# A hybrid decoder block on one core: adaLN's first part as TensorE products in column groups, and S5 without GpSimd

## The chip, the core and the metric

The kernel runs on one core of a Trainium2 chip. TensorE multiplies matrices into PSUM, VectorE (DVE) and ScalarE (ACT) do element work on SBUF and PSUM, GpSimd (POOL) does element work on SBUF alone, and SyncE (SP) issues most of the DMAs. Engines run side by side; each takes its own instructions in order. The metric is the device time of one execution in microseconds, as the median of several runs.

## The reference

One layer (sequence 512, model width 1024, batch 1) of a token mixer and a channel mixer. Cut to what the change touches:

```python
c_act = jax.nn.silu(c)
mod = c_act @ ada_w + ada_b                       # (1024) @ (1024 x 6144)
sh1, sc1, gt1, sh2, sc2, gt2 = split(mod, 6)
h = rms_norm(x, pre1_w) * (1.0 + sc1) + sh1       # sh1, sc1: "adaLN's first part"
z = h @ w_in                                      # one input projection for three branches
#  A: chunked gated linear attention   B: mLSTM   C: S5, a complex diagonal state space
y = (g0 * (A @ proj_gla) + g1 * (B @ proj_ml) + g2 * (C @ proj_s5)) @ w_out
x = x + (1.0 + gt1) * rms_norm(y, post1_w)
#  then the channel mixer: SwiGLU with its own shift, scale and gate
```

In S5 each group of 16 channels drives 64 complex states, `x_t = Abar x_{t-1} + Bbar u_t`, `y_t = Re(C x_t) + D u_t`, with `Abar` and `Bbar` computed from `lam`, `log_step` and `b`.

## The kernel before, in words

Large matrix products keep fp32's precision by splitting each operand into a `hi` half (rounded, on ScalarE) and a `lo` half (what is left, on VectorE or GpSimd) and adding three products: hi by hi, hi by lo, lo by hi (`passes`, lines 424 to 426; for products with tokens on the partitions, lines 456 to 458). Weights come through one stream (`Stream`): SP loads an item into a `raw` buffer (line 321), and `S.ahead(i, n)` splits the items up to `i + n`. In the opening the ring has nine raw buffers, later three.

The opening is laid out by hand: inside `head` the order on all engines is the order of the text, though small work of later stages (S5's parameters, named `w`) is put into it by the planner, which places all other instructions by its own costs and by the order in which they were written. The opening does this:

- TensorE runs products of ones by ones (`warm`, line 542, counts in `WARM`) while x comes in. The squares of x are summed, `r` is the reciprocal root, and `rb` its broadcast over partitions in PSUM (line 573).
- adaLN's first part has a matrix of 1024 by 2048, in 16 loads of 512 KB. The columns are cut into five `STRIPS` of 128 or 256. A load holds two or four slices along the contraction. Some loads (`NA` of each strip) are scaled on ScalarE and added on GpSimd (`ada_act`), the others are accumulated on VectorE (`ada_acc`); both end in an `acc` of 128 partitions.
- `prep(j)` sums `acc` over the partitions by products with a column of ones (line 589, and 591 for strip 0), which gives the scale and shift of the strip as columns, and forms `h` and the halves `hT` of its normed input from x, the columns and `rb`.
- `sweep(j)` multiplies the strip's `hT` into six PSUM banks (eight slices of the contraction in all, six groups of three products each). After `SWN[j]` groups it prepares the next strip.

Then follow the linear attention (seven levels of block masks, on VectorE, lines 1073 to 1097), S5 and mLSTM. Their own work is small, and large projections (`job`, run in pieces by `fill(n)`) stand between their steps, so that TensorE has work while the other engines prepare. S5's parameters (`s5_params`) give `bb` (a complex product on GpSimd) and the table of phases `ph` (one half of the columns on VectorE, the other on GpSimd). S5 runs over four blocks of eight groups: `params(b)` forms outer products (`outer`: of four products `o` two are VectorE's, two GpSimd's), sums them to `CA` and `wp`, multiplies small matrices in column groups of 32 (line 1239) and transposes; `states(b)` multiplies the inputs into states (line 1268), rotates them by `ph` (four products on VectorE, two adds on GpSimd), runs two scans on VectorE, rotates back (four products on GpSimd) and sums to `Xs`; `outputs(b)` gives the outputs. `rho` is copied to a tile on GpSimd.

After that come the merge of the branches, the output projection and the channel mixer, which the change doesn't touch.

Of the kernel before, what the change touches and what calls it, by code (L numbers as in the profile page):

```python
# [9 lines left out]
OP = mybir.AluOpType  # L10
# [5 lines left out]
STRIPS = ((0, 128), (1, 256), (3, 256), (5, 256), (7, 128))  # L16
# [150 lines left out]
PP = (1, 3, 5)  # L167
WARM = (17, 1, 2, 0, 7, 0, 7)
LEAD = 5
AB = (0, 0, 0)  # L170
NA = (1, 2, 2, 2, 1)
SWN = (3, 5, 5, 5, 0)
# [14 lines left out]
def _emit(tc, nc, ctx, ExitStack, A, out, act, dve, pool, pe, sp):  # L187
# [286 lines left out]
    def ada_act(dst, k0, n, more):  # L474

        def f(t):
            w = 1024 // n
            for i in range(n):
                sl = slice(i * w, (i + 1) * w)
                af(t[:, sl], t[:, sl], AF.Copy, scale=cact[:, k0 + i:k0 + i + 1])  # L480
            if n == 4:
                tt(pool, t[:, 0:512], t[:, 0:512], t[:, 512:1024], OP.add)
            a = dst()
            if more:
                tt(pool, t[:, 0:w], t[:, 0:w], t[:, w:2 * w], OP.add)
                tt(pool, a, a, t[:, 0:w], OP.add)
            else:
                tt(pool, a, t[:, 0:w], t[:, w:2 * w], OP.add)
        return f

    cact2 = const.tile([128, 8], F32, name="cact2")
    adas = {}
    strip_w, strip_a = [], []
    i = 0
    for j, (c0, w) in enumerate(STRIPS):
        n = 512 // w
        na = NA[j]
        strip_a.append(len(items))
        for z in range(8 // n):
            def dst(j=j, z=int(z >= na), w=w):  # L500
                if (j, z) not in adas:
                    adas[j, z] = slot("acc")
                return adas[j, z][:, 0:2 * w]

            def other(j=j, w=w):
                return adas[j, 0][:, 0:2 * w]

            add_item(A["ada0"][i], kind="ada", start=True,
                     acc=ada_act(dst, n * z, n, z > 0) if z < na else
                     ada_acc(dst, n * z, n, n * na, None, other if j else None))  # L510
            i += 1
        strip_w.append([add_item(A["sweep"][k], w=768, start=True, pool=k in PP) for k in range(c0, c0 + w // 128)])

# [23 lines left out]
    af(st[:, 0:1], epsc, AF.Sqrt)  # L537
# [8 lines left out]
    for i in range(4):  # L546
        warm(WARM[i], ones)
        sq = [slot("sq"), slot("sq")]
        for h in range(2):
            xh = xT[i][:, h * 512:(h + 1) * 512]  # L550
            if h and i == 2:
# [22 lines left out]
    warm(WARM[5], ones)  # L574
    S.ahead(1, 0)
# [3 lines left out]
    S.ahead(2, 0)  # L579
    S.ahead(strip_a[1] + NA[1] - 1, 0)  # L580
    sweep_ps = [mm_bank() for _ in range(4)] + [ax_bank() for _ in range(2)]

    def prep(j):
# [13 lines left out]
        for k in range(c0, c0 + n):  # L597
            hs[k] = slot("h")
            hT[k] = tuple(hTp.tile([128, 512], F32R, tag=f"{z}{k}", name="hT") for z in "hl")
            stt(hs[k], xT[k // 2][:, (k % 2) * 512:(k % 2 + 1) * 512], g1c[:, k:k + 1], rb, OP.mult, OP.mult)  # L600
            af(hT[k][0], hs[k], AF.Identity, bias=s1c[:, k:k + 1])
        for k in range(c0, c0 + n):
            stt(hT[k][1], hs[k], s1c[:, k:k + 1], hT[k][0].bitcast(F32), OP.add, OP.subtract)

    def sweep(j):

        for i, idx in enumerate(strip_w[j]):
            k = STRIPS[j][0] + i
# [245 lines left out]
    with head:  # L854
        prep(0)
        warm(WARM[6], ones)
# [874 lines left out]
```

## Time and profile before

| | us |
|---|---|
| runs | 949.90, 950.78, 953.11 |
| median | 950.78 |
| profiled execution | 952.81 |
| its span, first to last instruction | 950.9 |

The profiled execution is one of its own, and the rows below come from it. Times in it are microseconds from the start of its span. "Busy" is the time in which an engine has at least one instruction; TensorE's products overlap, so a product of 0.39 us can follow the one before it after 0.23. PEclk is the share of 2.4 GHz that was granted to TensorE; 0.50 is 1.2 GHz. DVE is VectorE, ACT ScalarE, POOL GpSimd, PE TensorE, SPq the DMA issues of SyncE.

### The profile page before, as it was taken

The numbers are of one execution on the slowest core, as the hardware profiler recorded it, in microseconds if no ns is written. First come the engines' busy times: TensorE is split into PE (matmuls) and PEld (weight loads), VectorE is DVE, ScalarE is ACT, GpSimd is POOL, SyncE is SP. The second block draws the span as 40 slices with busy tenths as digits, with TensorE's granted clock in tenths as the row PEclk, the third lists the DMA queues.
The fourth block names the chain that finished last, engine by engine and source line by source line (L and its number), as shares of the span: only waits on it lengthen the run. The fifth ranks groups of instructions, "written<-read, shape, count | busy, mean of one in ns | idle before, by whom it ended". The sixth has DMA issues, their size and how long they took to land.

```text
span 950.9 us, 11658 instructions
## 1 busy us (share of the span) xinstructions
PE 908.7 (96%) x4290; PEld 741.8 (78%) x4290; DVE 606.4 (64%) x1100; ACT 337.8 (36%) x519; POOL 168.8 (18%) x208
## 2 busy tenths in 40 slices
PE   9699999999888999999999998999999999999997
PEld 9577787777776787878888786788888888888885
DVE  4998998889798894595667779653343433322215
ACT  5338513432323444362333354522322323212113
POOL 4440005405235230221212223000000000000000
PEclk7799999999999999999999999999999999999999
DMA  9624242133433432243555733444243333333303
GB/s 365 218 81 130 90 144 66 35 113 112 148 112 112 127 110 78 89 137 108 177 175 167 237 131 133 154 156 132 89 141 126 110 108 114 111 97 104 110 1 133
DMA packets 52193, 120.80 MB, mean 127 GB/s; under 512 B 13796, under 2 KB 19428, under 8 KB 52136
## 3 DMA queue, kind: packets, MB, share of 16 engines
q1 hardware_dynamic: 49944, 115.92, 37.1%
q0 software_dynamic: 1040, 2.38, 1.0%
q10 hardware_dynamic: 1152, 1.75, 0.5%
q8 instruction: 34, 0.56, 0.3%
q14 instruction: 23, 0.19, 0.1%
HBM read 113.21 MB, written 6.82 MB: 126 GB/s over the span
## 4 chain that ended last, share of the span: by engine, by line
PE 51%; DVE 7%; DMA 3%; issue 1%; ACT 1%; POOL 0%; SPq 0%; DVEq 0%; ACTq 0%
PE mm L424 11%; PE mm L425 11%; PE mm L426 11%; PE y L1512 4%; PE y L1513 4%; PE y L1511 4%; DVE lo L222 1%; DMA raw<-ada 1%; DVE xn L228 1%; PE mm L456 1%; PE mm L457 1%; PE mm L458 1%; DVE st L228 1%; DVE xn L222 1%; DMA raw<-wout 1%
## 5 line engine op out<-in xcount | busy, mean ns | idle before, releaser
L231 ACT ACTIVATE hi<-raw 128x1024 fp32r<-128x1024 f32 (+2 forms) x157 | 151.7, 971 | 406.1 <-PE mm L425 161.0
L222 DVE TENSOR_TENSOR lo<-raw,hi 128x1024 fp32r<-128x1024 f32 (+2 forms) x151 | 180.9, 1200 | 163.7 <-ACT hi L231 163.1
L424 PE MATMUL mm<-h2hi,hi 128*128 128x512 f32 x320 | 124.7, 390 | 0.0
L426 PE MATMUL mm<-h2hi,lo 128*128 128x512 f32 x320 | 124.6, 389 | 0.0
L425 PE MATMUL mm<-h2lo,hi 128*128 128x512 f32 x320 | 124.5, 389 | 0.0
L426 PE MATMUL mm<-hT,lo 128*128 128x512 f32 x280 | 112.9, 403 | 9.2 <-DVE lo L222 9.2
L424 PE MATMUL mm<-hT,hi 128*128 128x512 f32 x280 | 114.0, 407 | 0.0
L425 PE MATMUL mm<-hT,hi 128*128 128x512 f32 x280 | 112.6, 402 | 0.3 <-DVE hT L228 0.3
L426 PEld LDWEIGHTS mm<-hT,lo 128*128 128x128 f32 x280 | 54.4, 194 | 22.3 <-DVE lo L222 10.5
L426 PEld LDWEIGHTS mm<-h2hi,lo 128*128 128x128 f32 x320 | 60.1, 188 | 12.6
L425 PEld LDWEIGHTS mm<-h2lo,hi 128*128 128x128 f32 x320 | 60.1, 188 | 12.4
L424 PEld LDWEIGHTS mm<-h2hi,hi 128*128 128x128 f32 x320 | 60.1, 188 | 12.3
L1513 PE MATMUL y<-hi,g 128*128 128x512 f32 x176 | 68.5, 389 | 0.0
L1512 PE MATMUL y<-lo,g 128*128 128x512 f32 x176 | 68.5, 389 | 0.0
L1511 PE MATMUL y<-hi,g 128*128 128x512 f32 x176 | 68.3, 389 | 0.0
L222 DVE TENSOR_TENSOR sg<-sg,mm 128x512 f32<-128x512 f32 x36 | 24.7, 685 | 67.7 <-PE mm L426 67.7
L425 PEld LDWEIGHTS mm<-hT,hi 128*128 128x128 f32 x280 | 54.6, 195 | 12.5 <-DVE hT L228 1.1
L424 PEld LDWEIGHTS mm<-hT,hi 128*128 128x128 f32 x280 | 54.7, 195 | 12.0 <-issue 0.5
L228 DVE SCALAR_TENSOR_TENSOR gacc<-raw,cact,gacc 128x512 f32<-128x512 f32 x56 | 45.0, 803 | 21.7 <-DMA raw<-ada 21.0
L456 PE MATMUL mm<-hi,hT 128*128 128x512 f32 x128 | 50.5, 401 | 2.3 <-ACT mo L231 2.3
L457 PE MATMUL mm<-lo,hT 128*128 128x512 f32 x128 | 50.0, 391 | 0.0
L458 PE MATMUL mm<-hi,hT 128*128 128x512 f32 x128 | 49.5, 392 | 0.0
(322 smaller groups left out, 1598.0 us busy)
## 6 DMA issues: line engine op xcount, KB each, us to landing
raw<-ada SPq DMA_DIRECT2D x48, 512.0 KB, 3.4
raw<-ffn SPq DMA_DIRECT2D x44, 512.0 KB, 3.4
raw<-wzg SPq DMA_DIRECT2D x24, 512.0 KB, 3.4
raw<-ffo SPq DMA_DIRECT2D x22, 512.0 KB, 3.2
raw<-wpr SPq DMA_DIRECT2D x24, 256.0 KB, 2.8
raw<-wout SPq DMA_DIRECT2D x8, 512.0 KB, 5.8
raw<-sweep SPq DMA_DIRECT2D x8, 384.0 KB, 7.5
xT<-xT SPq DMA_DIRECT2D x4, 512.0 KB, 5.3
```

The source lines that it names most:

```text
L222: e.tensor_tensor(out=o, in0=a, in1=b, op=op)
L228: dve.scalar_tensor_tensor(out=o, in0=a, scalar=s, in1=b, op0=op0, op1=op1)
L231: act.activation(out=o, in_=i, func=f, **kw)
L424: mm(ps, lhsT=whi, rhs=xhi, start=first, stop=False)
L425: mm(ps, lhsT=whi, rhs=xlo, start=False, stop=False)
L426: mm(ps, lhsT=wlo, rhs=xhi, start=False, stop=last)
L456: mm(ps[t], lhsT=xh[:, tk], rhs=hi[:, sl], start=(k == 0), stop=False)
L457: mm(ps[t], lhsT=xh[:, tk], rhs=lo[:, sl], start=False, stop=False)
L458: mm(ps[t], lhsT=xl[:, tk], rhs=hi[:, sl], start=False, stop=(k == 7))
L1511: mm(ps, lhsT=xhi, rhs=whi[:, sl], start=first, stop=False)
L1512: mm(ps, lhsT=xhi, rhs=wlo[:, sl], start=False, stop=False)
L1513: mm(ps, lhsT=xlo, rhs=whi[:, sl], start=False, stop=last)
```

## The change

adaLN's first part is computed by TensorE: for each slice `k` of the contraction a product with 32 weight columns, the first of which is the activated `c` and the others zero (`cz`), put at column group `32 * (k % 4)`, so that four slices write four groups of partitions of one bank. ScalarE copies the bank to SBUF (`evac`), and the products with a column of ones in `prep` sum the groups as they summed the partitions before. The strips are cut as 128, 128, 256, 256, 256, and `SWN` now says after how many groups the next strip's loads are multiplied (two halves) and prepared; `sweep` yields ahead of each group instead of behind it. All splits of the opening are VectorE's. Sixteen of 34 warm-up products are left out. `rb` is copied to SBUF after the first strip. In S5 the products and adds of GpSimd go to VectorE, in part as fewer and wider instructions, and the copies of `rho` to ScalarE; the table of phases, so far built by halves on two engines, is built whole on VectorE. In the diff's last parts stand, in this order, `prep`, the loop of the opening, `s5_params`, `outer` and `states`.

```diff
-STRIPS = ((0, 128), (1, 256), (3, 256), (5, 256), (7, 128))
+STRIPS = ((0, 128), (1, 128), (2, 256), (4, 256), (6, 256))
-PP = (1, 3, 5)
-WARM = (17, 1, 2, 0, 7, 0, 7)
+WARM = (17, 1, 0, 0, 0, 0)
-NA = (1, 2, 2, 2, 1)
-SWN = (3, 5, 5, 5, 0)
+SWN = ((0, 0, 2), (0, 2, 3), (2, 4, 6), (2, 4, 6))
...
+    cz = G[:, 0:256].rearrange("p (k m) -> p k m", k=8)
+    def ada_pe(j, k0, n, w):
         def f(t):
+            if k0 == 0:
+                ada_ps[j] = ax_bank("ab")
             for i in range(n):
+                k = k0 + i
+                q = 32 * (k % 4)
+                mm(ada_ps[j][q:q + 32, 0:2 * w], lhsT=cz[:, k], rhs=t[:, i * 2 * w:(i + 1) * 2 * w],
+                   start=(k < 4), stop=(k >= 4), tile_position=(0, q))
...
-    sp.dma_start(out=ident, in_=A["ident"])
     S.load()
     S.load()
+    sp.dma_start(out=ident, in_=A["ident"])
     sp.dma_start(out=pv, in_=A["pv"])
+    pool.memset(cz, 0.0)
...
+    cp(cz[:, :, 0:1], cact.unsqueeze(2))
...
+    af(st[:, 16:17], epsc, AF.Sqrt)
     warm(WARM[4], ones)
-    S.ahead(0, 0)
+    S.ahead(strip_a[0][-1], 0)
...
+    def evac(j):
+        n = 2 * STRIPS[j][1]
+        ada_sb[j] = slot("ae")
+        af(ada_sb[j][:, 0:n], ada_ps.pop(j)[:, 0:n], AF.Copy)
+    evac(0)
...
-            mm(cb[:, i:i + 1], lhsT=adas[j, 1][:, sl], rhs=ones[:, 0:1], start=True, stop=(j > 0))
+            mm(cb[:, i:i + 1], lhsT=ada_sb[j][:, sl], rhs=ones[:, 0:1], start=True, stop=True)
...
+        if j == 0:
+            rbs[0] = slot("rbs")
+            af(rbs[0], rb, AF.Copy)
...
     with head:
+        S.ahead(strip_w[0][-1], 0)
         prep(0)
-        warm(WARM[6], ones)
+        warm(WARM[5], ones)
         for j in range(len(STRIPS)):
             for n, _ in enumerate(sweep(j)):
-                if n == SWN[j] and j + 1 < len(STRIPS):
-                    S.ahead(strip_w[j + 1][-1], 0)
-                    if j + 2 < len(STRIPS):
-                        S.ahead(strip_a[j + 2] + AB[j], 0)
+                for z in range(2):
+                    if n == SWN[j][z]:
+                        S.ahead(strip_a[j + 1][z], 0)
+                if n == SWN[j][1]:
+                    evac(j + 1)
+                if n == SWN[j][2]:
                     prep(j + 1)
...
-        cmul(bb[:, 0], bb[:, 1], sv[:, 0], sv[:, 1], b16(zr), b16(zi), w16(xs5), w16(ys5), pool)
+        cmul(bb[:, 0], bb[:, 1], sv[:, 0], sv[:, 1], b16(zr), b16(zi), w16(xs5), w16(ys5))
...
-                     bc(u_r), bc(u_i), w(xs5), w(ys5), pool if a else dve)
+                 bc(u_r), bc(u_i), w(xs5), w(ys5))
...
-            tt(pool if i % 2 else dve, w(x[i]), pb(m), ab(n), OP.mult)
+            tt(dve, w(x[i]), pb(m), ab(n), OP.mult)
...
-        cp(r3, rho[:, 4 * b:4 * b + 4].unsqueeze(2).broadcast_to([128, 4, 64]), pool)
+        for z in range(2):
+            af(r3[:, 4 * z:4 * z + 4], rho[:, 4 * b:4 * b + 4].unsqueeze(2).broadcast_to([128, 4, 64]), AF.Copy)
-        tt(dve, x[:, re], ps[:, re], pr_, OP.mult)
-        tt(dve, x[:, im], ps[:, im], pr_, OP.mult)
-        tt(dve, y[:, re], ps[:, im], pi_, OP.mult)
-        tt(dve, y[:, im], ps[:, re], pi_, OP.mult)
-        tt(pool, w[:, re], x[:, re], y[:, re], OP.add)
-        tt(pool, w[:, im], x[:, im], y[:, im], OP.subtract)
+        tt(dve, z2(x), z2(ps), pr_, OP.mult)
+        tt(dve, z2(y), z2(ps)[:, ::-1], pi_, OP.mult)
+        tt(dve, w[:, re], x[:, re], y[:, re], OP.add)
+        tt(dve, w[:, im], x[:, im], y[:, im], OP.subtract)
-        for s_ in (re, im):
-            dve.tensor_tensor_scan(out=v[:, s_], data0=rh[:, 0:256], data1=w[:, s_], initial=0.0,
-                                   op0=OP.mult, op1=OP.add)
+        dve.tensor_tensor_scan(out=v, data0=rh, data1=w, initial=0.0, op0=OP.mult, op1=OP.add)
-        tt(pool, x[:, re], v[:, re], pr_, OP.mult)
-        tt(pool, x[:, im], v[:, im], pr_, OP.mult)
-        tt(pool, y[:, re], v[:, im], pi_, OP.mult)
-        tt(pool, y[:, im], v[:, re], pi_, OP.mult)
+        tt(dve, z2(x), z2(v), pr_, OP.mult)
+        tt(dve, z2(y), z2(v)[:, ::-1], pi_, OP.mult)
```

## Rows read from the trace of the kernel before

**Rows 1.** The page's first section: busy time of an engine in us, its share of the span, and its instructions.
```profile
PE 908.7 (96%) x4290; PEld 741.8 (78%) x4290; DVE 606.4 (64%) x1100; ACT 337.8 (36%) x519; POOL 168.8 (18%) x208
```

**Rows 2.** The list of TensorE's waits over the whole span, the two longest in total: who waited, for whom, us in total, times, and the longest in us.
```profile
PE mm L426 <- DVE lo L222: 10.7, 4, 4.7
PE ax L589 <- DVE acc L222: 9.4, 3, 4.2
```

**Rows 3.** The table by stretch, in the opening: from and to in us, length, busy time and instructions of PE, PEld, DVE, ACT and POOL, granted clock, share of the DMA engines, GB/s.
```profile
10.30:23.90 13.60, 13.60 (x66) 13.60 (x65) 7.74 (x31) 7.21 (x16) 5.82 (x5) 0.50 1.03 405
...
27.50:30.70 3.20, 0.00 (x0) 0.00 (x0) 3.18 (x9) 0.00 (x0) 0.23 (x1) 1.00 0.35 113
30.80:37.50 6.70, 6.48 (x19) 5.30 (x20) 5.77 (x19) 3.37 (x6) 0.68 (x1) 0.50 0.86 307
...
40.90:44.40 3.50, 0.00 (x0) 0.00 (x0) 3.48 (x5) 0.00 (x0) 2.63 (x2) 1.00 0.85 260
44.50:51.20 6.70, 6.17 (x19) 5.24 (x20) 5.81 (x21) 3.02 (x5) 0.33 (x1) 0.50 0.40 156
...
59.10:77.30 18.20, 18.20 (x84) 14.74 (x84) 17.02 (x64) 6.88 (x9) 2.97 (x7) 1.00 0.64 193
```

**Rows 4.** The timeline of TensorE in the opening: start in us, us, engine, line, operation, out<-in, form, count, and in brackets the idle time before it with what ended it. L542 are warm-up products, L589 the column products, L424 to L426 the sweep's.
```profile
14.36 3.33 PE L542 MATMUL ax<-ones 128*128 128x128 f32 x14
...
23.74 0.58 PE L424 MATMUL mm<-hT,hi 128*128 128x512 f32 x1
...
34.15 0.63 PE L424 MATMUL ax<-hT,hi 128*128 128x512 f32 x1
34.58 0.63 PE L425 MATMUL ax<-hT,hi 128*128 128x512 f32 x1
...
59.07 1.02 PE L589 MATMUL ax<-ones,acc 128*128 128x1 f32 x8 [1.65 <-DVE acc L222]
...
60.27 0.39 PE L425 MATMUL mm<-hT,hi 128*128 128x512 f32 x1
60.50 0.40 PE L426 MATMUL mm<-hT,lo 128*128 128x512 f32 x1
...
77.05 0.39 PE L426 MATMUL ax<-hT,lo 128*128 128x512 f32 x1
```

**Rows 5.** The table by stretch again, columns as in rows 3: the attention, the S5 stage, and two short stretches of the S5 stage.
```profile
77.00:165.00 88.00, 85.00 (x432) 69.43 (x432) 81.32 (x231) 41.59 (x54) 16.05 (x42) 1.00 0.31 98
...
205.00:330.00 125.00, 111.38 (x683) 90.23 (x682) 103.56 (x151) 39.90 (x52) 43.75 (x49) 0.96 0.39 123
...
242.40:245.80 3.40, 3.40 (x9) 2.64 (x8) 1.20 (x2) 0.89 (x1) 0.00 (x0) 0.50 0.66 232
...
303.80:307.20 3.40, 2.83 (x7) 2.25 (x8) 3.31 (x6) 0.00 (x0) 1.69 (x2) 0.51 0.42 154
```

**Rows 6.** Groups of instructions in the first 64 us, by form: line, engine, operation, out<-in, form, count, then busy us and mean ns of one, then idle us before them.
```profile
L228 DVE SCALAR_TENSOR_TENSOR acc<-raw,cact,acc 128x512 f32<-128x512 f32 x9 | 10.4, 1152 | 0.0
...
L222 DVE TENSOR_TENSOR lo<-raw,hi 128x768 fp32r<-128x768 f32 x4 | 3.8, 953 | 0.1
...
L222 POOL TENSOR_TENSOR raw<-raw 128x512 f32<-128x512 f32 x5 | 6.9, 1376 | 23.2 <-ACT raw L231 23.2
L222 POOL TENSOR_TENSOR lo<-raw,hi 128x768 fp32r<-128x768 f32 x3 | 6.3, 2089 | 1.1 <-ACT hi L231 1.1
```

**Rows 7.** The timeline of TensorE around S5's products in column groups (L1239, weights of 32 columns), and around sixteen untiled fp32 passes of the attention (L1092). Columns as in rows 4.
```profile
210.35 0.64 PE L1239 MATMUL ax<-CA,bs 128*32 128x128 f32 x16
210.92 0.55 PE L1254 MATMUL ax<-ident,wp 128*128 128x128 f32 x3
...
101.62 1.95 PE L1092 MATMUL ax<-Qp,K 128*128 128x128 f32 x16
103.32 0.48 PE L456 MATMUL mm<-hi,hT 128*128 128x512 f32 x1
```

**Rows 8.** The timelines of VectorE and of GpSimd in one block of S5. Columns as in rows 4.
```profile
225.37 1.23 DVE L222 TENSOR_TENSOR o<-pw,bb 128x512 f32<-128x512 f32 x1
...
230.12 2.91 DVE L228 SCALAR_TENSOR_TENSOR CA<-o,o 64x512 f32<-64x512 f32 x2
233.06 0.69 DVE L222 TENSOR_TENSOR o<-pw,bb 128x512 f32<-128x512 f32 x1
...
236.78 1.38 DVE L222 TENSOR_TENSOR wp<-o,o 64x512 f32<-64x512 f32 x2
...
224.87 1.18 POOL L222 TENSOR_TENSOR y<-v,ph 128x256 f32<-128x256 f32 x1
...
229.50 2.97 POOL L222 TENSOR_TENSOR o<-pw,bb 128x512 f32<-128x512 f32 x2
```

**Rows 9.** Groups of GpSimd's instructions from 64 to 350 us, by form. Columns as in rows 6.
```profile
L222 POOL TENSOR_TENSOR o<-pw,bb 128x512 f32<-128x512 f32 x8 | 11.6, 1459 | 7.5 <-DVE CA L222 7.5
...
L222 POOL TENSOR_TENSOR w<-x,y 128x256 f32<-128x256 f32 x8 | 6.2, 796 | 74.1 <-DVE y L222 74.1
```

**Rows 10.** DMA issues of the first 80 us: out<-in, queue, operation, count, KB each, median us from issue to landing.
```profile
raw<-ada SPq DMA_DIRECT2D x16, 512.0 KB, 6.2
```

More of the change, by code (lines that the diff above doesn't have):

```diff
@@ L496, in _emit, with ada_items, sweep_items @@
         n = 512 // w
[L497 to L512, printed above, removed]
+        def ada_items():
+            first = len(items)
+            for z in range(8 // n):
+                add_item(A["ada0"][i + z], kind="ada", start=True, acc=ada_pe(j, n * z, n, w))
+            return [first + 4 // n - 1, first + 8 // n - 1]
+        def sweep_items():
+            return [add_item(A["sweep"][k], w=768, start=True) for k in range(c0, c0 + w // 128)]
+        if j == 0:
+            strip_a.append(ada_items())
+            strip_w.append(sweep_items())
+        else:
+            strip_w.append(sweep_items())
+            strip_a.append(ada_items())
+        i += 8 // n
     act.dma_start(out=cT, in_=A["c"])
@@ L536, in _emit @@
     af(cact, cT, AF.Silu)
-    af(st[:, 0:1], epsc, AF.Sqrt)
+    cp(cz[:, :, 0:1], cact.unsqueeze(2))
     wb = ax_bank()
@@ L550, in _emit @@
             xh = xT[i][:, h * 512:(h + 1) * 512]
-            if h and i == 2:
+            if h and i % 2:
                 tt(dve, sq[h], xh, xh, OP.mult)
@@ L573, in _emit @@
         mm(rb[:, tk], lhsT=ones, rhs=rd[:, tk], start=True, stop=True)
-    warm(WARM[5], ones)
-    S.ahead(1, 0)
     ts(dve, adab1, P("ada_b"), 1.0, None, OP.add)
     stt(cact2, r[:, 0:1].broadcast_to([128, 8]), 0.0, cact, OP.mult, OP.add)
-    S.ahead(2, 0)
-    S.ahead(strip_a[1] + NA[1] - 1, 0)
-    sweep_ps = [mm_bank() for _ in range(4)] + [ax_bank() for _ in range(2)]
+    ada_sb = {}
+    def evac(j):
[3 more added lines that the diff above has]
+    evac(0)
+    rbs = [rb]
     def prep(j):
@@ L854, in _emit @@
     with head:
+        S.ahead(strip_w[0][-1], 0)
         prep(0)
[L856 removed]
+        warm(WARM[5], ones)
+        sweep_ps += [mm_bank() for _ in range(4)] + [ax_bank() for _ in range(2)]
         for j in range(len(STRIPS)):
             for n, _ in enumerate(sweep(j)):
[L859 to L862 removed]
+                if j + 1 == len(STRIPS):
+                    continue
+                for z in range(2):
[4 more added lines that the diff above has]
+                if n == SWN[j][2]:
                     prep(j + 1)
@@ L865, in _emit @@
         act.dma_start(out=s5c.rearrange("p z a c -> p (z a c)"), in_=A["s5c"])
-        S.ahead(strip_w[-1][-1] + HB, 0)
+        S.ahead(strip_a[-1][-1] + HB, 0)
     startp.close()
@@ L1270, in states @@
         fill(2)
-        pr_, pi_ = (ph[:, z, 4 * b:4 * b + 4].rearrange("p a n -> p (a n)") for z in range(2))
+        z2 = lambda a: a.rearrange("p (z n) -> p z n", z=2)
+        pr_, pi_ = (ph[:, z, 4 * b:4 * b + 4].rearrange("p a n -> p (a n)").unsqueeze(1).broadcast_to([128, 2, 256])
+                    for z in range(2))
         rh = slot("rho")
-        r3 = rh[:, 0:256].rearrange("p (a n) -> p a n", n=64)
-        cp(r3, rho[:, 4 * b:4 * b + 4].unsqueeze(2).broadcast_to([128, 4, 64]), pool)
+        r3 = rh.rearrange("p (z a n) -> p (z a) n", z=2, n=64)
+        for z in range(2):
+            af(r3[:, 4 * z:4 * z + 4], rho[:, 4 * b:4 * b + 4].unsqueeze(2).broadcast_to([128, 4, 64]), AF.Copy)
         pool.memset(r3[:, :, 0:1], 0.0)
```

31 lines of the change are left out of this document (8 added, 23 removed).

## The prediction

> **What bounds the kernel now.** I read the page's busy times first: TensorE is at work for 96% of the span, VectorE for 64%, GpSimd for 18% [rows 1]. So most of the time is TensorE's own products, and a change that adds no products can only give back the places where TensorE waits or runs slowly. The list of waits says where these are [rows 2]: 9.4 us in three waits for adaLN's sums (`acc`, the column products of line 589) and 10.7 us in four waits for the `lo` half of a split weight. The first belong to the opening stage, the others to the S5 stage.
>
> The table by stretch then gives the opening [rows 3]. TensorE has nothing to do from 27.5 to 30.7 and from 40.9 to 44.4 us, VectorE is full in both, and after each pause the granted clock stands at 0.50 for 6.7 us (1.2 instead of 2.4 GHz). The timeline of TensorE gives the ends [rows 4]: the first sweep product starts at 23.74, the last at 77.05, and at the full clock one follows another after 0.233 us (60.27 to 60.50). The sweep has 144 products, 33.6 us of work, and takes 53.5: 9.4 of waits, 4.7 of column products (1.6, 1.7, 0.9 and 0.4, from their starts to the next product), some 4.3 where about 22 products ran in the slow stretches at 0.43 us each (34.15 to 34.58 [rows 4]), and 1.5 in small pieces.
>
> In the S5 stage (205 to 330 us) TensorE is idle for 13.6 of 125 us while VectorE is busy for 103.6 and GpSimd for 43.8 [rows 5]. Three pauses there are followed by a stretch of some 3.4 us at half the clock (the first and the last of them in [rows 5]).
>
> **The opening, part by part.** *Removed:* adaLN's first part on three engines, 10.4 us of VectorE's wide accumulations at 1152 ns each and 6.9 us of GpSimd's halving adds [rows 6], with ScalarE's scalings; GpSimd's three `lo` splits go to VectorE, where one takes 0.95 us instead of 2.09 [rows 6]. All of this leaves the path, since the waits for `acc` stood behind it.
>
> *Added on TensorE:* 16 loads of 1024 columns, as fp32 products with 32 weight columns on four column groups. The nearest row is line 1239, which has this shape (128x32 weights, fp32, four groups): 8 products of 128 columns, in 16 passes, start at 210.35, and the next, untiled product starts at 210.92 [rows 7]. That is 0.57 us for 1024 columns, going in and out of the tiled mode included; untiled, 16 passes of 128 columns go from 101.62 to 103.32, 1.70 us [rows 7]. The four loads of strips 0 and 1 run at the half clock, some 4 us, partly in the shadow of the norm and of `h`, so little of them is on the path. The other 12 go into the sweep, between its groups: 12 x 0.57 = 6.8, less the switches saved where two loads come together; I take 6.5. Bounds: 5.2 (no switch at all) and 20.4 (no overlap of groups, 12 x 1.70).
>
> The Trainium skill, "TensorE: Matmul & The Clock Gate", section "Measured speedup vs the span model", gives 2.38x for three column tiles; an estimate by that efficiency would be 3.2x for four, 1.7 us more than row 1239 makes of the twelve loads. The row measures this very form, so I keep the row.
>
> *Column products* remain: 0.9 us for each of three strips at the full clock, about 0.6 for strip 1: 3.3. *Evacuation* is a ScalarE copy of 512 columns per strip, some 0.7 us, for which two sweep groups (1.4 us) stand ahead of `prep` in strips 3 and 4, but only one (0.7) in strip 2: a wait of about 0.4 there. `prep` itself (three small adds, two `h`, ScalarE's `hT`, `lo`) is some 2.8 us against three groups of 2.1 in strip 2 and six groups in the later ones: another 0.7. With small pieces I put 1.5 for waits.
>
> *Queues.* On SP `ident` moves behind two loads and the order of loads changes with the strips. The opening loads 13.9 MB (16 loads of 512 KB for adaLN [rows 10], the weights of the sweep and x); 405 GB/s were moved in 10.3 to 23.9 [rows 3], so the last adaLN load can land after about 36 us, or some 42 with waits for free buffers, and is wanted at about 50. GpSimd's queue gets one memset and loses all its work here. ScalarE gains five evacuations and one copy of `rb`, and loses the scalings; its Sqrt table load moves behind the squares, where ScalarE is idle. The first adaLN products of strip 1 may need the bank of `rb`, so they may wait for its copy; the sweep then starts at 23.8 instead of 21.6. I take 22.5.
>
> *Warm-up products:* 16 of 34 go, among them 7 before the norm (14 passes, 3.3 us) and 7 ahead of the sweep (the first of these two in [rows 4]). Without the last ones I expect the sweep to begin at the half clock and to reach the full one about 27: 2.6 us lost there.
>
> The sum from the sweep's first product: 33.6 + 6.5 + 3.3 + 1.5 + 2.6 = 47.5, so it ends at 70.0 instead of 77.3. The opening gives 7.5 us. Bounds: 11 (start at 21.6, full clock early, loads at 5.2, hardly a wait) and 3 (start at 23.8, one more slow stretch, 3 us of waits).
>
> **S5 on VectorE.** The rows show that the two engines do not work side by side on such operands. While GpSimd is in a 256-wide product of 1.18 us (`y`, 224.87), VectorE's 512-wide product takes 1.23 (225.37); alone it takes 0.69 (233.06) [rows 8]. Beside GpSimd's 512-wide products (229.50, 2.97 for two) two 64x512 operations take 2.91, alone 1.38 (236.78) [rows 8]. So GpSimd's wide product costs VectorE about 0.77 us, its narrow one 0.54. Per block four wide ones, four narrow ones and two adds go (x8 for each of the wide ones' two operand sets and for the adds, in four blocks [rows 9]), giving back 3.1 + 2.2 + 0.6 = 5.9. VectorE takes on four products of 0.61 to 0.69, two of 512 for `x` and `y`, and two adds at 0.34 to 0.42: 4.3 to 5.0. The merged PSUM products and the one scan in place of two change little; `rho` goes to ScalarE, busy for 39.9 of the 125 us [rows 5]. So a block's stretch gets 0.9 to 1.6 us shorter, though most of GpSimd's 43.8 us are gone, and the splits behind it come earlier by that. The stretch is hidden where TensorE has filler work, and ends a wait otherwise. Three blocks with 1.6 us less and one slow stretch fewer (3.4 us at 0.43 instead of 0.233 a product, 1.5 lost) give 6; the order may eat some of it; I take 5. Bounds: 18 (all 13.6 us of waits and three slow stretches at 1.5 gone) and a loss of 13 (all four blocks pay about 4.3 with nothing given back, less some slack).
>
> `bb` and the phase table run in the attention's stage, where VectorE is busy for 81.3 and TensorE for 85.0 of 88 us [rows 5]. They add some 6 us to VectorE there, and about as much is given back by the same lock; I put 0.5 us of loss (bounds: 1 gained, 3 lost).
>
> **Sum.** -7.5 - 5 + 0.5 = -12. The profiled execution took 952.81 us with a span of 950.9, 1.9 around it; the median of the three runs is 950.78, 2.0 below it. The forecast is 940.8 for an execution like the profiled one, and 939 on the median.
>
> **Rivals.** *S5 gives back everything:* the waits vanish with the lock: 950.8 - 7.5 - 18 = 925. For it: VectorE has idle time between the blocks. Against: its work per block hardly shrinks.
>
> *Only the opening gains:* sixteen products in a row are ready on VectorE at once, so the planner puts splits behind them as late as before: 943 to 946.
>
> *VectorE becomes the bound of S5 and attention:* the moved work adds waits of 8 us, which eat the opening: about 951. Rows 8 speak against it.
>
> *The clock (slower):* place, the sweep; price, 0.194 us for each product. If the tiled products, the column products and the short waits leave the granted clock at half through the sweep, 144 products take 61.5 us, twelve loads 12 and the column products 6: it ends at 22.5 + 81 = 103, 26 late, so with S5's gain about 972. It decides against the change from some 60 slow products on, where the 12 us are gone. For it: from 10.3 to 23.9 TensorE was busy for all 13.6 us and the clock stood at 0.50 [rows 3]. Against: from 59.1 on 1.00 was granted throughout, right after a wait of 1.65 us [rows 3, 4], and no wait that I expect is longer.
> The Trainium skill, the same page, section "Why this matters for your kernels", wants TensorE kept busy without pauses and warmed up; by it, leaving out warm-up products costs. The first of these rows differs from it as far as the profile's word busy goes.
>
> *The groups do not run together:* 20.4 us instead of 6.5 in the sweep, so 953. Line 1239 speaks against it.
>
> **How the numbers follow.** The forecast as worked out (933 to 945) has 0.62, S5 in full 0.08, the opening alone 0.14, VectorE as the bound 0.07, the clock 0.06, the groups one after another 0.03. A measurement can tell about 0.3%, 2.9 us, so faster means under 947.9: 0.84; the same 0.05 (most of VectorE as the bound); slower 0.11. The range runs from 927 (10 from the opening and 14 from S5) to 950 (3 from the opening, 2 lost in S5).
>
> **What would show it.** Right: the last sweep product at about 70; no wait for `acc`; a pair of adaLN loads in about 1.1 us; the clock at 1.00 from about 27 on; S5's 512-wide products at 0.69 and its three pauses shorter by one to two us each. Wrong: slow stretches inside the sweep, waits over 1.5 us at the strips' borders, or S5 pauses as long as now.

## The result and the profile after

The changed kernel takes 929.25 us (median of four runs, 927.30 to 930.82), the kernel before, run beside it, 951.64: a ratio of 0.9764, with a 95% interval of 0.9738 to 0.9791. That is 22.4 us less; 12 were forecast. The profiled execution took 930.82 with a span of 929.0, 21.9 less than the span before.

The page's busy times, which answer to [rows 1]:

```profile
PE 904.5 (97%) x4334; PEld 732.4 (79%) x4334; DVE 581.3 (63%) x1108; ACT 336.6 (36%) x515; POOL 75.3 (8%) x100
```

GpSimd lost 93.5 us of work, and VectorE, which took over most of it, is busy for 25 us less. In the opening that is adaLN, now TensorE's; in S5 it is the subject of the experiments.

TensorE's timeline in the opening, for [rows 4] (L556 the norm's sums, L485 adaLN's loads, L593 the column products, L422 to L424 the sweep):

```profile
8.69 3.86 PE L556 MATMUL ax<-ones,sq 128*128 128x1 f32 x24
12.47 1.93 PE L485 MATMUL ab<-raw,G 128*32 128x256 f32 x16
14.38 2.08 PE L573 MATMUL ax<-rd,ones 128*128 128x128 f32 x8
16.24 0.85 PE L593 MATMUL ax<-ones,ae 128*128 128x1 f32 x4
17.02 1.93 PE L485 MATMUL ab<-raw,G 128*32 128x256 f32 x16
19.19 0.80 PE L422 MATMUL mm<-hT,hi 128*128 128x512 f32 x1 [0.24 <-ACT hT L229]
...
26.28 1.06 PE L485 MATMUL ab<-raw,G 128*32 128x512 f32 x8
27.28 0.50 PE L422 MATMUL mm<-hT,hi 128*128 128x512 f32 x1
27.61 0.40 PE L423 MATMUL mm<-hT,hi 128*128 128x512 f32 x1
...
66.13 0.40 PE L424 MATMUL ax<-hT,lo 128*128 128x512 f32 x1
```

And the table by stretch, with the columns of [rows 3]:

```profile
12.40:19.20 6.80, 6.56 (x46) 3.88 (x46) 5.75 (x35) 3.36 (x9) 0.00 (x0) 0.50 1.03 406
19.20:23.70 4.50, 4.50 (x12) 3.42 (x13) 4.07 (x23) 1.43 (x3) 0.00 (x0) 0.50 1.03 406
23.70:66.40 42.70, 42.34 (x210) 28.43 (x208) 27.95 (x97) 15.59 (x21) 2.71 (x7) 1.00 0.64 227
```

The sweep runs from 19.19 to 66.13; before, from 23.74 to 77.05. From 23.7 on TensorE hardly stops (42.3 of 42.7 us busy, one wait of 0.4) and keeps the full clock.

TensorE's waits from 190 to 352 us:

```profile
PE mm L454 <- ACT mo L229: 4.1, 3, 2.5
PE mm L424 <- DVE lo L220: 3.1, 1, 3.1
```

The kernel before had the four waits for `lo` of [rows 2] there, 10.7 us, one of 2.3 for `mo`, and two more in S5:

```profile
PE mm L424 <- DVE merged L222: 1.6, 1, 1.6
PE ax L1239 <- DVE bs L234: 1.3, 1, 1.3
```

So S5 has one pause of 3.1 us, where it had six with 13.6 in sum. VectorE's forms in that stage (192 to 320 us), for [rows 8]:

```profile
L220 DVE TENSOR_TENSOR o<-pw,bb 128x512 f32<-128x512 f32 x12 | 8.0, 687 | 0.1
L220 DVE TENSOR_TENSOR o<-pw,s5c 128x512 f32<-128x512 f32 x12 | 7.4, 681 | 0.0
...
L226 DVE SCALAR_TENSOR_TENSOR CA<-o,o 64x512 f32<-64x512 f32 x6 | 4.1, 686 | 0.1
```

Before, in the same stage (204.4 to 341.3 us):

```profile
L222 DVE TENSOR_TENSOR o<-pw,s5c 128x512 f32<-128x512 f32 x6 | 7.9, 1354 | 0.0
L222 DVE TENSOR_TENSOR o<-pw,bb 128x512 f32<-128x512 f32 x6 | 7.1, 1204 | 0.1
...
L228 DVE SCALAR_TENSOR_TENSOR CA<-o,o 64x512 f32<-64x512 f32 x6 | 5.6, 940 | 0.1
```

Since the planner orders S5 anew for each kernel, I compare by marks that every trace has: the first and the last product of the sweep, the last transpose of the attention's `og`, and the first product of the output projection. "Middle" is the stretch between the last two of these; S5 lies in it. All in us from the span's start of the one profiled execution of each kernel; the first column is the median of its runs.

| kernel | time | sweep begins | sweep ends | og done | output projection | middle |
|---|---|---|---|---|---|---|
| before | 951.64 | 23.74 | 77.05 | 204.40 | 525.08 | 320.7 |
| after | 929.25 | 19.19 | 66.13 | 192.13 | 502.73 | 310.6 |
| opening alone | 940.23 | 18.28 | 64.72 | 190.44 | 512.57 | 322.1 |
| tables and S5 alone | 937.79 | 23.82 | 78.69 | 205.12 | 513.05 | 307.9 |
| `outer` on two engines | 936.32 | 17.84 | 64.30 | 189.30 | 508.11 | 318.8 |
| `states` on two engines | 936.55 | 17.96 | 64.92 | 191.17 | 507.90 | 316.7 |
| idle products, early | 929.38 | 18.23 | 67.38 | 193.43 | 501.13 | 307.7 |
| idle memsets | 928.46 | 17.98 | 66.06 | 192.13 | 500.25 | 308.1 |
| `ffn0`'s splits on VectorE | 927.83 | 18.16 | 65.36 | 191.40 | 502.28 | 310.9 |
| warm-up ahead of the norm | 928.16 | 19.77 | 65.23 | 191.27 | 497.51 | 306.2 |
| 16 idle products in S5 | 944.81 | 18.06 | 64.44 | 193.79 | 515.27 | 321.5 |
| 16 narrow ones | 928.84 | 17.91 | 64.87 | 190.97 | 501.44 | 310.5 |
| one column group | 943.43 | 23.64 | 84.52 | 210.54 | 517.05 | 306.5 |
| the version of the end | 922.78 | 21.53 | 67.01 | 193.03 | 499.28 | 306.2 |

With S5 as changed, the middle lies between 306 and 311 us, whichever order the planner finds. So a difference of up to 5 us in this column can be the order alone, except between kernels with the same order. Against the kernel before, the change gained 10.9 us in the opening, 1.3 in the attention and 10.1 in the middle. The middle by stretch (columns as in [rows 3]), before and after:

```profile
204.40:525.08 320.68, 304.77 (x1577) 246.63 (x1577) 239.56 (x349) 117.79 (x166) 89.00 (x95) 0.98 0.40 127
```

```profile
192.13:502.73 310.60, 303.26 (x1576) 246.14 (x1576) 232.09 (x364) 123.95 (x177) 45.12 (x57) 0.99 0.42 131
```

TensorE stands idle for 15.9 us of it before and for 7.3 after: 8.6 of the 10.1 us are waits, and 1.5 are a shorter busy time.

### The profile page after: what moved, and what is told of

It reads as the page before. It is cut to its first block, busy times and chain, and to the rows that moved or that the text cites. A ratio compares the mean times of both kernels' runs of the same rounds, so it can differ in the third digit from the quotient of the medians.

```text
span 929.0 us, 11608 instructions
## 1 busy us (share of the span) xinstructions
PE 904.5 (97%) x4334; PEld 732.4 (79%) x4334; DVE 581.3 (63%) x1108; ACT 336.6 (36%) x515; POOL 75.3 (8%) x100
## 3 DMA queue, kind: packets, MB, share of 16 engines
q0 software_dynamic: 1040, 2.38, 1.0%
## 4 chain that ended last, share of the span: by engine, by line
PE 52%; DVE 5%; DMA 4%; ACT 2%; issue 1%; POOL 0%; SPq 0%; DVEq 0%; ACTq 0%
PE mm L422 11%; PE mm L424 11%; PE mm L423 11%; PE y L1520 4%; PE y L1521 4%; PE y L1519 4%; DMA raw<-ada 2%; DVE lo L220 1%; ACT L229 1%; DVE st L226 1%; DMA raw<-wout 1%; DVE gacc L226 1%; PE mm L455 1%; PE mm L456 1%; PE mm L454 1%
## 5 line engine op out<-in xcount | busy, mean ns | idle before, releaser
L422 PE MATMUL mm<-h2hi,hi 128*128 128x512 f32 x320 | 124.7, 390 | 0.0
L424 PE MATMUL mm<-h2hi,lo 128*128 128x512 f32 x320 | 124.6, 389 | 0.0
L424 PE MATMUL mm<-hT,lo 128*128 128x512 f32 x280 | 111.2, 397 | 3.1 <-DVE lo L220 3.1
L422 PE MATMUL mm<-hT,hi 128*128 128x512 f32 x280 | 113.1, 404 | 0.2 <-ACT hT L229 0.2
L423 PE MATMUL mm<-hT,hi 128*128 128x512 f32 x280 | 111.2, 397 | 0.4 <-DVE hT L226 0.4
L424 PEld LDWEIGHTS mm<-h2hi,lo 128*128 128x128 f32 x320 | 60.1, 188 | 12.5
L422 PEld LDWEIGHTS mm<-h2hi,hi 128*128 128x128 f32 x320 | 60.1, 188 | 12.2
L422 PEld LDWEIGHTS mm<-hT,hi 128*128 128x128 f32 x280 | 53.7, 192 | 16.5 <-issue 3.4
L424 PEld LDWEIGHTS mm<-hT,lo 128*128 128x128 f32 x280 | 53.5, 191 | 14.9 <-DVE lo L220 3.5
L423 PEld LDWEIGHTS mm<-hT,hi 128*128 128x128 f32 x280 | 53.5, 191 | 11.8 <-DVE hT L226 1.2
L226 DVE SCALAR_TENSOR_TENSOR gacc<-raw,cact,gacc 128x512 f32<-128x512 f32 x56 | 42.9, 767 | 21.3 <-DMA raw<-ada 20.5
L454 PE MATMUL mm<-hi,hT 128*128 128x512 f32 x128 | 50.6, 405 | 4.1 <-ACT mo L229 4.1
```

What stands on the lines that cost most here:

```text
L226: dve.scalar_tensor_tensor(out=o, in0=a, scalar=s, in1=b, op0=op0, op1=op1)
L422: mm(ps, lhsT=whi, rhs=xhi, start=first, stop=False)
L423: mm(ps, lhsT=whi, rhs=xlo, start=False, stop=False)
L424: mm(ps, lhsT=wlo, rhs=xhi, start=False, stop=last)
L454: mm(ps[t], lhsT=xh[:, tk], rhs=hi[:, sl], start=(k == 0), stop=False)
```

## The experiments

Theory: the opening's gain is TensorE's column groups and an earlier, unbroken sweep; S5's gain is that GpSimd no longer holds VectorE. Rivals: the gains need each other; S5's gain is the planner's order or VectorE's load; the groups do not run together; warm-up products set the start.

**Each part alone.** One kernel has the diff up to the loop of the opening, the other what follows it (`s5_params`, `outer`, `states`).

> Only the opening of the change (adaLN's first part on TensorE, the new strips, most warm-up products left out); the attention's tables and S5 as before. Theory: each part acts at its own place and the gains add, so this has the whole gain up to the last sweep product, 10.9 us, and nothing behind it: the last sweep product at 66.1, the last outputs of S5 (341.3 before) at about 330.4, the time 951 - 11 = 940. Rival: part of what came later (the 10 us between the sweep and the end of S5) also came from the opening, because everything behind it meets its loads and buffers earlier: then 932 to 936. Second rival: the gain of the opening needs the rest and is eaten in S5's waits: 945 to 949.

> Only the later part of the change (the attention's tables and S5 without GpSimd); the opening as before. Theory: the gains add, so this gives the 11 us that the changed kernel gained behind the sweep: about 940, the last S5 outputs about 10 us earlier than in the kernel before, S5's pauses for lo of 2 us and less except one. Rival: the later part gives the 5 us of the prediction and the other 5 came with the opening: 946. Second rival: it gives all 20: 930.

Measured: 940.23 and 937.79, against 954.5 of the kernel before, run beside them: 0.9851 (0.9828 to 0.9874) and 0.9825 (0.9798 to 0.9852). By spans, 939.4 and 937.8 us: 11.5 and 13.1 less than before, 24.6 in sum, against 21.9 for both. The table says where: the opening alone ends its sweep 12.3 us early and has the middle of the kernel before (322.1); S5 alone has the opening of before and a middle of 307.9. Each part acts at its own place, and both rivals of each fall. S5 alone gives more than the 5 us of the prediction. How exactly the two add is not shown: by the medians, with the kernel before at 954.5 beside them and at 951.64 beside the changed kernel, they give 31.0 us in sum against 22.4.

**One half of S5 back.**

```diff
-            tt(dve, w(x[i]), pb(m), ab(n), OP.mult)
+            tt(pool if i % 2 else dve, w(x[i]), pb(m), ab(n), OP.mult)
```

> The changed kernel with two of the four 512-wide products of each S5 outer product back on GpSimd (16 instructions in all). Theory (the lock): what GpSimd takes off VectorE it takes back by holding it: 16 x 0.68 = 10.9 us leave VectorE and 16 x 0.77 = 12.3 us come back in longer instructions, and the two in a row on GpSimd make each outer product end later. So S5 ends 1 to 4 us later and the time is 930 to 934; VectorE's wide products beside GpSimd's at about 1.2 to 1.35 us instead of 0.69. Rival (VectorE's load): fewer instructions on VectorE bring its splits earlier: 925 to 928.

The other kernel has the last part of the diff (`states`) undone.

> The changed kernel with the states' step back as it was (rho's copy, two adds and four narrow products of each block on GpSimd, four narrow PSUM products and two scans on VectorE). Theory (the lock): it is the narrow products and the adds that hold VectorE 2.2 + 0.6 us a block, more than they save, so this costs 2 to 6 us: 931 to 935, and the pauses for lo come back. Rival: the merged VectorE form adds what it removes, so nothing changes: 928 to 930. With the run before it: what the two cost together should come near the 11 us that the later part gained, less what the tables gave.

Measured: 936.32 (0.9805, 0.9779 to 0.9831) and 936.55 (0.9813, 0.9789 to 0.9837), where the changed kernel has 0.9764. By the table the middle is 8.2 us longer with `outer` back and 6.1 with `states` back, where the theory asked for 1 to 4 and 2 to 6. TensorE's waits with `outer` back, from 189 to 350 us:

```profile
PE mm L424 <- DVE lo L220: 4.5, 2, 2.4
PE ax L1250 <- DVE bs L232: 3.1, 1, 3.1
PE mm L422 <- DVE merged L220: 1.0, 1, 1.0
...
```

The pauses are back, though VectorE has 16 products less: VectorE's load as the reason falls. But both kernels were ordered anew, and 8.2 + 6.1 is more than the 10.1 that the whole change gained, so the order has a share in these numbers. The next runs are made to keep it out.

**Products on GpSimd that nobody waits for.** Behind the memset of `bs` four were added in each block, and four memsets in the control:

```diff
         pool.memset(bs[:, 0:256], 0.0)
+        one4 = ones.unsqueeze(1).broadcast_to([128, 4, 128])
+        for _ in range(4):
+            tt(pool, G[:, 0:512].rearrange("p (a n) -> p a n", n=128), one4, one4, OP.mult)
```

> The changed kernel with four 512-wide products added on GpSimd in each S5 block (16 in all, both operands from SBUF, into a buffer that nothing reads before it is written anew), behind the memset of bs. Nothing waits for them. The run beside it has 16 memsets of the same buffer in their place, and the same order of instructions on TensorE and ScalarE, so the two differ only in what GpSimd does. Theory (the lock): each product holds VectorE back by 0.77 to 0.86 us, up to 13 us over the four blocks; with the slack of the stage 4 to 9 us longer than with the memsets. Rival (the order that the planner finds, or VectorE's load, made S5's gain, not the lock): within 1.5 us of the run with the memsets.

> The control to the run before: 16 memsets of 128x512 on GpSimd, 0.52 us each, where that one has products. A memset reads no operand; theory: VectorE's 512-wide products stay at 0.69 us and the time is that of the changed kernel, 927 to 932, with what the new order in S5 makes of it (1 to 3 us either way). Rival (any work of GpSimd holds VectorE): 2 to 5 us more, 16 x 0.3 us.

Measured: 929.38 and 928.46, no difference; but the run does not test the theory. The products depend on nothing, the planner let GpSimd run them ahead, and in the trace they lie at 51.8 to 74.4 us, in the sweep and just behind it. There VectorE's two `hT` (0.75 us each elsewhere in that opening) took 2.97 together, and TensorE waited 0.75 for them; beside the control's memsets the same two took 1.42. So the products were then tied to S5:

```diff
             tt(dve, w(x[i]), pb(m), ab(n), OP.mult)
+            if i == 0:
+                for _ in range(2):
+                    tt(pool, G[:, 0:512], x[0][:, 0:512], x[0][:, 0:512], OP.mult)
```

The control has 16 columns for 512. In the traces ScalarE's order is the same in both; TensorE's differs in 10 of 4334 products and VectorE's in 13 of 1108 instructions, by the names of their tiles, all from 303 us on. The control has the order of the changed kernel on all three engines.

> In the run with independent products on GpSimd these had run long before S5, so it said nothing of S5. Here two 512-wide products on GpSimd read the first product of each outer product (16 in all) and so run while VectorE works on the rest; nothing waits for their result. The run beside it has the same 16 with 16 columns, and nearly the same order on every engine. Theory (the lock): each holds VectorE by about 0.8 us, 12 to 13 us over four blocks; S5's end comes 4 to 9 us later than beside it, the pauses for lo grow by as much, VectorE's products beside them take 1.2 to 1.5 us. Rival (S5's gain came from the order and from VectorE's load): S5's end within 1.5 us of the run beside it.

> The control to the run before: 16 products of 16 columns on GpSimd. Theory: the fixed part of such an instruction holds VectorE little, so 927 to 931, S5's end about as in the changed kernel (254 us after the last sweep product). Rival (the hold does not depend on the width): as long as the run before.

Measured: 944.81 (0.9906, 0.9873 to 0.9938) and 928.84 (0.9751, 0.9728 to 0.9775). Sixteen products that no one waits for cost 16 us by the medians, seven tenths of all that the change gained; one of the six runs with them took only 935.94, the others 943.19 to 946.49, and nothing here says why. The timeline of VectorE with them, in one block (start, us, and so on as in [rows 4]):

```profile
216.89 0.68 DVE L220 TENSOR_TENSOR x<-v,ph 128x512 f32<-128x512 f32 x1
...
218.09 1.29 DVE L220 TENSOR_TENSOR o<-pw,bb 128x512 f32<-128x512 f32 x2
...
219.90 2.13 DVE L220 TENSOR_TENSOR CA<-o,o 64x512 f32<-64x512 f32 x2
222.06 2.87 DVE L226 SCALAR_TENSOR_TENSOR CA<-o,o 64x512 f32<-64x512 f32 x2
```

And GpSimd's beside it:

```profile
214.71 11.12 POOL L220 TENSOR_TENSOR G<-o 128x512 f32<-128x512 f32 x4 [11.75 <-DVE o L220]
```

With 16 columns, VectorE at the same place:

```profile
217.32 1.38 DVE L220 TENSOR_TENSOR CA<-o,o 64x512 f32<-64x512 f32 x2
218.73 1.39 DVE L226 SCALAR_TENSOR_TENSOR CA<-o,o 64x512 f32<-64x512 f32 x2
```

Four `CA` take 5.0 us instead of 2.8; three of them are held, 0.75 us each, as in [rows 8]. In both kernels GpSimd's first product of this block begins while VectorE runs 512-wide products back to back, and does not get on until the first `CA`: its lengths are 6.77 and 5.95 us, the second for 16 columns. The stage by stretch (columns as in [rows 3]), first with the wide products, then with the narrow ones:

```profile
193.80:334.50 140.70, 131.78 (x775) 108.63 (x774) 121.03 (x184) 45.25 (x64) 29.34 (x26) 0.93 0.37 118
```

```profile
191.00:319.00 128.00, 124.88 (x775) 103.64 (x774) 110.92 (x182) 44.97 (x64) 24.56 (x26) 0.98 0.43 130
```

VectorE is busy for 10.1 us more with hardly any more work (twelve of the sixteen products lie here), the stage is 12.7 us longer, and the granted clock falls from 0.98 to 0.93: beside TensorE's pauses of 4.1 us for `og` and 6.4 for `lo` lie 6.8 us each at 0.50, behind one of 1.5 for `wp` 10.2. Between the two profiled executions the spans differ by 13.3 us (941.4 and 928.1): 3.3 of them lie in the attention, where the first block's four products are, and 11.0 in the middle. VectorE is busy for 11.4 us more in all (593.9 for 582.5). So a product that holds VectorE for some 0.7 us costs 0.8 of the time in these two executions, and 1.0 by the medians. The memsets of the first control held nothing, as the two `hT` beside them showed. The Trainium skill says the same in "SBUF — State Buffer", section "Who interferes with whom": a VectorE instruction with two inputs in SBUF collides with a GpSimd instruction that reads SBUF, not with one that only writes. The traces agree on both halves, with 0.75 us of hold for a GpSimd product and 1.42 us for two `hT` beside memsets.

**The same hold far from S5.** Behind the output projection the order of TensorE, VectorE and ScalarE is written by hand. In the changed kernel GpSimd still has three splits there. VectorE's timeline, and GpSimd's:

```profile
546.34 0.15 DVE L301 RECIPROCAL st<-st 128x1 f32<-128x1 f32 x1
546.52 4.72 DVE L226 SCALAR_TENSOR_TENSOR st<-st 128x1 f32<-128x1 f32 x2
```

```profile
546.46 4.77 POOL L220 TENSOR_TENSOR lo<-raw,hi 128x1024 fp32r<-128x1024 f32 x2 [2.03 <-ACT hi L229]
```

Two steps on a single column take as long as GpSimd's two splits. The edit gives the splits to VectorE:

```diff
-    ffn0_i = [tail_item(A["ffn0"][u], pool=u != 2) for u in range(4)]
+    ffn0_i = [tail_item(A["ffn0"][u], pool=False) for u in range(4)]
```

> The changed kernel with the three lo splits behind the gated output (ffn0, 128x1024, 2.4 us each on GpSimd) on VectorE too. The order there is written by hand and stays as it is on TensorE and ScalarE. Theory (the lock works on any VectorE instruction, not on wide products alone): two steps on a single column took 2.37 and 2.32 us on VectorE at 546.5 and 548.9 beside these splits, and TensorE then waited 2.15 us for h2lo and 2.33 us for lo; both waits go to under 1 us, the columns take 0.2 us, and the time falls by 2 to 5 us: 924 to 927. Rival (VectorE is loaded by 3 x 1.2 us more at this place, so the waits stay): 929 to 931.

Measured: 927.83 (0.9740, 0.9708 to 0.9772). The waits from 500 to 570 us were 2.3 for GpSimd's `lo`, 2.1 for `h2lo`, 0.8 and 1.1 in three small ones; now they are:

```profile
PE ax L1573 <- POOL xn L220: 1.7, 1, 1.7
PE ax L1602 <- DVE lo L220: 1.2, 2, 0.7
...
PE y L1520 <- DVE lo L220: 0.8, 1, 0.8
```

The two single-column steps take 0.41 us, though VectorE has 3.7 us of work more, and the stretch from the output projection's first product to `ffn0`'s first is 1.5 us shorter (49.1 for 50.6). What remains is GpSimd's next instruction, the add of `xn`. By the time alone, 1.4 us where 2 to 5 were expected, it would not be told from no change.

**Warm-up products.**

```diff
-WARM = (17, 1, 0, 0, 0, 0)
+WARM = (17, 1, 0, 0, 7, 0)
```

> The changed kernel with 7 warm-up products (14 passes) put back ahead of the norm's products, as the kernel before had them. Theory: these passes stood in TensorE's queue ahead of the norm's products (3.1 us there, from 14.36 to 17.48), and leaving them out is what brought the sweep's start from 22.5 forecast to 19.2; so the sweep starts at 22 to 22.7 and the time is 2 to 3.5 us more, 931.5 to 933, less what a clock that rises earlier gives back. Rival: the start is set by the loads of x, by ScalarE or by the loads of adaLN: it stays under 20 and the time at 929. Second rival: the passes lift the clock to full before the sweep: start at 20.5, the first products at 0.23 us instead of 0.43, time 928 or less.

Measured: 928.16 (0.9756, 0.9724 to 0.9787). TensorE's timeline (L541 are the warm-up products):

```profile
11.21 2.79 PE L541 MATMUL ax<-ones 128*128 128x128 f32 x14
13.93 1.69 PE L485 MATMUL ab<-raw,G 128*32 128x256 f32 x16
...
16.98 1.07 PE L485 MATMUL ab<-raw,G 128*32 128x256 f32 x16
19.77 0.50 PE L422 MATMUL mm<-hT,hi 128*128 128x512 f32 x1 [1.72 <-ACT hT L229]
```

The second rival holds in the main. The passes take 2.7 us, but behind them the clock is full (strip 1's loads in 1.07 instead of 1.93 us) and stays so; the sweep begins 0.6 to 1.9 us later than in the openings without them (17.84 to 19.19), takes 45.5 us instead of 46.4 and more, and ends at 65.23. So leaving these seven out neither gained nor lost, and my theory of what brought the start forward falls. What did is earlier: in the twelve profiles with the changed opening VectorE begins the norm's reduction, behind the last sum, at 11.2 to 12.6 us, in the two with the old one at 14.5 and 14.6. A part of the reason is on ScalarE. Before:

```profile
4.84 1.28 ACT L231 ACT_TABLE_LOAD   x1
...
6.24 1.13 ACT L231 ACTIVATE sq<-xT 128x512 f32<-128x512 f32 x2
```

After:

```profile
4.71 1.65 ACT L229 ACTIVATE sq<-xT 128x512 f32<-128x512 f32 x3
...
8.90 1.28 ACT L229 ACT_TABLE_LOAD   x1
```

The squares start 1.5 us earlier because Sqrt's table is loaded behind them, and VectorE takes two of eight where it took one. But they end only 0.6 to 1.1 us earlier (10.1 to 10.5 us for 11.1); the larger part is TensorE's. In the kernel before VectorE had the squares done and then waited 3.4 us for TensorE's sums, which stood behind four warm-up passes and ran at a clock of 0.50 from 10.3 us on [rows 3]:

```profile
10.18 1.11 PE L542 MATMUL ax<-ones 128*128 128x128 f32 x4
...
11.08 3.41 PE L557 MATMUL ax<-ones,sq 128*128 128x1 f32 x16
```

```profile
14.53 0.17 DVE L561 TENSOR_REDUCE st<-ax 128x4 f32<-128x16 f32 x1 [3.39 <-PE ax L557]
```

With the changed opening that wait is 1.1 to 2.4 us. The four passes (0.9 us to the next sum) are among the sixteen left out, and this run does not put them back. No run moves the table load or these passes alone, so how the earlier start divides between them and the clock is not settled.

**All slices in one column group.**

```diff
-                q = 32 * (k % 4)
+                q = 0
...
-                   start=(k < 4), stop=(k >= 4), tile_position=(0, q))
+                   start=(k == 0), stop=(k == 7), tile_position=(0, q))
```

The copy and the column products then read 32 rows.

> The changed kernel with adaLN's eight products of each strip all in the first column group, one behind the other, summed there (the evacuation and the column products then read 32 rows). Theory (four groups run side by side at no price): a pair of loads in the sweep takes 2 x 1.70 = 3.4 us instead of 1.0, six pairs 14 us more, and the loads of strips 0 and 1 up to 2 x 1.5 us more at half the clock, partly hidden: the last sweep product at 80 to 83, the time 943 to 947. Rival (the efficiency of 2.38 for three groups that the Trainium skill gives in TensorE: Matmul & The Clock Gate, section Measured speedup vs the span model, holds here, so groups give some 3.2 and each load would already cost 0.53 of 1.70): the pair takes 3.2 us against 1.06; hardly to be told apart by the time, but by the pair's own duration. Second rival (the loads are hidden behind other waits of the sweep): under 936.

Measured: 943.43 (0.9901, 0.9878 to 0.9924); the sweep takes 60.9 us instead of 46.9. A pair of loads in it:

```profile
33.91 3.62 PE L485 MATMUL ab<-raw,G 128*32 128x512 f32 x8
37.46 0.51 PE L422 MATMUL mm<-hT,hi 128*128 128x512 f32 x1
```

That is 3.55 us to the next product; on four groups it is 1.00 (26.28 to 27.28), changes of mode included: a factor of 3.5. The 2.38 for three groups of the Trainium skill ("TensorE: Matmul & The Clock Gate", section "Measured speedup vs the span model") would make 3.2 an estimate for four; the runs go by more, for 512 fp32 columns. The theory stands: six pairs at 2.55 us more make 15.3, and the sweep is 14.0 longer. It also begins 4.5 us later, behind strip 0's loads; the time is only 14.2 longer because the middle, ordered anew, is 4.1 shorter.

**A faster version.** The splits of `ffn0` and the adds of `xn` on VectorE, and the seven warm-up products:

```diff
-WARM = (17, 1, 0, 0, 0, 0)
+WARM = (17, 1, 0, 0, 7, 0)
-    ffn0_i = [tail_item(A["ffn0"][u], pool=u != 2) for u in range(4)]
+    ffn0_i = [tail_item(A["ffn0"][u], pool=False) for u in range(4)]
-            tt(dve if h else pool, xn[t][h], xn[t][h], SG[h], OP.add)
+            tt(dve, xn[t][h], xn[t][h], SG[h], OP.add)
```

> A version meant to be faster than the changed kernel: the three lo splits of ffn0 and the adds of xn on VectorE too, and 7 warm-up products ahead of the norm. Theory: the waits for h2lo (2.15), lo (2.3) and xn (1.7 in the run with the splits alone) go, 3 to 5 us with the slow stretch behind them; the warm-up products cost 2.7 us and give as much back by the clock: 924 to 927. Rival: VectorE's load at that place brings the waits back: 928 to 930.

Measured: 922.78 (0.9689, 0.9666 to 0.9712), 6.5 us under the changed kernel; its interval lies wholly under that one's. By stages, of the 9.0 us between the two profiled spans: 3.3 us between the output projection and `ffn0`, 2.2 behind, 4.4 in the middle, whose order is that of the run with the seven products (306.2 both times), and 0.9 lost in the opening. The waits from 500 to 570 us now:

```profile
PE ax L1573 <- DVE st L223: 0.8, 1, 0.8
PE ax L1573 <- DVE xn L220: 0.7, 1, 0.7
PE ax L1602 <- DVE lo L220: 0.7, 1, 0.7
...
```

## Why the prediction was right, and where its sizes were off

*What bounds the kernel, and that both parts gain:* right. The two alone gave 11.5 and 13.1 us of span. The size is another matter: the time lies in the range (927 to 950), but outside the 933 to 945 that had 0.62. Opening, attention and S5 all gave more than forecast, and the sum came within 2.3 us of the range's end. Of the rivals, that S5 gives back everything (18 us, chance 0.08) came about by more than half: 10.5 of S5's 13.6 us of pauses went. The others did not.

*The sweep (47.5 forecast, 46.9 measured):* right by its terms. Six pairs took 1.0 us each, 6 in all (6.5); the column products 0.7, 0.9, 0.8 and 0.8, 3.2 (3.3); the one wait inside 0.4 (1.5); the half clock lasted to 23.7 instead of 27 (2 us for 2.6). What the sum had not: the product behind a pair of loads is followed after 0.33 us instead of 0.23 (27.28 to 27.61), as is the one behind the wait (34.76 to 35.10). The groups' price from line 1239 [rows 7] held. One line of the working is wrong, though nothing hangs on it: 20.4 us over 3.2 is 6.4, which is 0.4 less than the 6.8 of row 1239 for twelve loads, and not 1.7 more.

*The start (22.5 forecast, 19.2 measured): the first mis-sized term.* It makes 3.3 of the 3.9 us by which the sweep ended before the 70.0 of the forecast. I had read that Sqrt's table load moves behind the squares, "where ScalarE is idle", and named no price for it, nor for the four warm-up passes between the sums. The norm was on the path: the squares end 0.9 us earlier, the passes had taken 0.9, and the sums end 2 us earlier. Strip 1's loads did not wait for the copy of `rb`, for which I had put 0.9 (22.5 for 21.6). The prediction shows no working for the 21.6 itself, so how much of the 2 us it held already is not known.

*The attention (+0.5 forecast, -1.3 measured):* the tables cost nothing. The stretch from the sweep's end to `og` is 126.0 us after, 125.7 with the tables as before and the new opening, 126.4 with the new tables and the old opening, 127.3 before. Which of them gives the 1.3 us is not settled.

*S5 (-5 forecast, -10.1 measured): the second mis-sized term.* The mechanism is right: VectorE's instructions fell to 0.69 us, and by stretch it is busy for 3.8 us less in S5 (114.6 us from 204.4 to 341.3 before, 110.8 from 192 to 320 after), where I had 0.9 to 1.6 for each of four blocks. The step that failed is the next one, from VectorE's time to TensorE's: I let three blocks give 1.6 us each and one slow stretch. But six pauses with 13.6 us became one with 3.1, and over the whole middle TensorE's waits fell by 8.6. The idle products show that VectorE's time can cost more than itself: in the middle 8.4 us more of VectorE (241.3 for 232.8) made 11.0 us more of time, 5.8 of them waits and 5.2 a longer busy time, with 9.8 us more at half the clock. By that rate, 1.3, the 3.8 us make 5.0. The rest up to 10.1 stays open: it is no more than what the planner's order alone moves (306 to 311 in the table), and no run here keeps the old order with the new work.

*The clock:* no slow stretch inside the sweep from 23.7 on. The row that spoke for this rival, full work at half the clock, came again ahead of the sweep (12.4 to 23.7). Between 10 and 25 us the clock was at half for 13.7 us in this profile and for 6.8 to 10.2 in nine others of openings without the seven warm-up products; with them, for 3.4 and 6.8 in two.

## What to carry to other kernels

Price work on GpSimd by what it does to VectorE, not by GpSimd's own time: an instruction that reads SBUF costs the time even where nothing waits for its result, as soon as VectorE is what TensorE waits for next. A quick test is to add such instructions, tied to the stage in question, and beside them the same number that are narrow. And when a piece of work moves, follow what moves up behind it: a table load and four warm-up passes out of the way of the norm were on the path, and the prediction named no price for either.

## What the runs showed of the hardware

- GpSimd can be shut out: in one block, while VectorE ran 512-wide products 0.60 us apart, each 0.69 long, a GpSimd product of 16 columns took 5.95 us, and 0.62 behind it.
- A VectorE step on one column took 2.4 us beside a GpSimd split of 128x1024, and 0.2 without it: the hold strikes steps of one column as well as wide products.
- Four column groups of 32 did the work of 3.55 us in 1.00.
- With adaLN's loads, the norm's products and column products alone (12.4 to 19.2), TensorE was busy for 6.6 of 6.8 us at a granted clock of 0.50.
